# Attention stage of a diffusion layer: transposes into two one-bank buffers, keys loaded by one transfer each, a projection spread over more of the stage

## The chip, the cores and the metric

The kernel runs on one core of a Trainium2 chip. A core has TensorE (matmuls, PE in the profile, its weight loads PEld), VectorE (DVE), ScalarE (ACT), GpSimd (POOL) and SyncE (SP), which here only issues transfers; 16 DMA engines carry all transfers. The metric is the device time of one execution in microseconds (us).

## The reference, cut to what matters

One layer over 1024 tokens and 256 context tokens with 16 heads of 64: an input projection, a recurrent branch, a neighbourhood attention, a merge of the two, and a mixture of 16 experts. The change lies in the attention and in the product of the recurrent branch that is computed beside it:

```python
s_loc = jnp.einsum('bjqhd,brjkhd->bhjqrk', qr, kb).astype(jnp.float32) * scale
s_loc = jnp.where(col_ok[:, :, None, :], s_loc + bias, NEG_INF)
s_ctx = jnp.einsum('bjqhd,bkhd->bhjqk', qr, k_ctx).astype(jnp.float32) * scale
p = jax.nn.softmax(jnp.concatenate([s_loc, s_ctx], axis=-1), axis=-1).astype(v.dtype)
o = (jnp.einsum('bhjqrk,brjkhd->bjqhd', p_loc, vb)
     + jnp.einsum('bhjqk,bkhd->bjqhd', p[..., n_loc:], v_ctx))
...
mix = jax.nn.sigmoid(gr) * (y_rnn @ w_proj_rnn[l]) + jax.nn.sigmoid(gn) * (y_na @ w_proj_na[l])
```

## The kernel before, in words

The stages follow each other: setup and input projections (to about 387 us), the recurrent branch (to 846 us), the attention (846 to 1214 us), the merge, and the experts (from about 1440 us to the end). Every product is made of three fp32r matmuls from high and low parts.

In the attention stage (`stage_attn`) the work is cut into 128 units: 8 pairs of heads, 8 strips of 128 queries, and the 2 heads of the pair. A unit sees 640 keys, or 512 in the first and the last strip; 96 units have 640. `attend` runs one step for each unit n, and the engines take the instructions in the order in which the steps issue them:

- `score(n)`: four matmuls (L905) into `sp`, two PSUM banks wide, of which columns 256 to 895 are used; DVE adds the bias and takes the maximum (L909), then negates it (L911).
- `turn(n - 3)`: four or five transposes on PE (L932) of the softmaxed tile `e` into `pt` (640 columns, two banks, one buffer), and one ACT copy to `et` (L934).
- `values(n - 5)`, at every second step: 20 or 16 matmuls (L949) of two units into `pv`; at the end of each half of a pair ACT and DVE split it (L955, L957) and POOL's queue stores it.
- `expo(n)`: the exponential on ACT (L917). At the next step's start `scale(n - 1)` divides by the sum on DVE (L923, L924).

`load_head` (q: L864; k: L869), `load_bias` (L882) and `load_v` (L876) issue the next pair's loads on SP's queue at steps 2, 4, 6 and 8 of a pair. Of the keys each head has two parts, `k0` and `k1`. A part is 64 rows of 1280 numbers in DRAM (`d_k`) and is wanted twice, in partitions 0 to 63 and 64 to 127: two transfers of 64 partitions each. Four heads fit at a time.

`project` computes the recurrent branch's projection beside it: 2 halves of the tokens by 8 column groups of 24 matmuls into `pr`. Each half begins with four 1 MB loads (`fetch`, L1012), each group needs a 256 KB gate tile (L1021), and each second group takes a 1 MB weight (`S.take8`, ring loads at L90, split by ACT and DVE). `weave` runs whichever of the two generators has the lower running total `done`; so `done` in `project` says at which step of `attend` its pieces of 6 matmuls stand.

Earlier, in the input projections, `out_parts` stores q and k by transfers whose DRAM side has four entries outermost (L484):

```python
nc.sync.dma_start(raw(dst.bitcast(F32), (g * 512 + o + part * 32) * width + tok,
                      [[128 * width, 4], [width, 32], [1, n]]), h[:, :n].bitcast(F32))
```

Of the kernel before, what the change touches and what calls it, by code (L numbers as in the profile page):

```python
# [12 lines left out]
F32 = mybir.dt.float32  # L13
# [12 lines left out]
NT = SEQ + CTX  # L26
# [27 lines left out]

SKIP1, SKIP2 = 7, 7
IDLE = 1
A1, A2 = 3, 4

LRU_ORDER = ([("in", 0)] + [e for j in range(1, 6) for e in (("in", j), ("gate", j - 1))]
# [3 lines left out]
def raw(t, off, dims):  # L63
    return bass.AP(tensor=t.tensor, offset=t.offset + off, ap=dims)
# [109 lines left out]
class Kernel:  # L174
# [142 lines left out]
    def stage_qkv(self):  # L317
# [169 lines left out]
        def mod_rows():  # L487
# [3 lines left out]
            def load(i):  # L491
                if i < 16:
                    ws.append(pl.tile([128, 2048], F32, name="wmr", tag="wmr", bufs=2))
                    nc.gpsimd.dma_start(ws[-1], I["wm"][8 + i])

            load(0)
            load(1)
            for _ in range(IDLE):
                yield
# [348 lines left out]
    def stage_attn(self):  # L848
        nc, I, S = self.nc, self.I, self.S
        self.hip2, self.c_hip2 = self.open_("hip2", side="right", bufs=1)  # L850
        p, cp = self.open_("attn", side="right", bufs=1)
# [4 lines left out]
        ps, cps = self.open_("psa", bufs=1, space=PSUM)  # L856
        L = {}

        def load_head(h):
            if h >= HEADS:  # L860
                return
            pool = pl if h % 4 < 2 else pk
            q = pool.tile([128, SEQ], F32R, name="q", tag="q", bufs=2)
            nc.sync.dma_start(q.bitcast(F32), self.d_q[h].bitcast(F32))  # L864
            ks = []
            for part in range(2):
                t = pool.tile([128, NT], F32R, name=f"k{part}", tag=f"k{part}", bufs=2)
                for x in range(2):
                    nc.sync.dma_start(t[x * 64:(x + 1) * 64].bitcast(F32),  # L869
                                      self.d_k[h, part * 64:(part + 1) * 64].bitcast(F32))  # L870
                ks.append(t)
            L["h", h] = (q, ks)
        def load_v(h):
            if h < HEADS:
                v = (po if h % 4 else pb).tile([128, 10, 128], F32, name="v", tag="v")
                nc.sync.dma_start(v, raw(self.d_v, (h // 2) * 128, [[D, 128], [128 * D, 10], [1, 128]]))  # L876
                L["v", h // 2] = v
# [7 lines left out]
        def keys(s):  # L885

            if s == 0:
                return 256, 0, 512, ((256, 0, 256), (512, SEQ, 256)), (0, 1, 8, 9)
            if s == 7:
                return 256, 896, 512, ((256, SEQ, 256), (512, 6 * 128, 256)), (8, 9, 6, 7)  # L890
            return 256, 256, 640, ((256, SEQ, 256), (512, (s - 1) * 128, 384)), (8, 9, s - 1, s, s + 1)

        units = [(pr, s, i) for pr in range(8) for s in range(8) for i in range(2)]
        state = {}

        def score(n):
            pr, s, i = units[n]
            h = 2 * pr + i
            q, ks = L["h", h]
            b = L["b", h]  # L900
            c0, b0, w, segs, tiles = keys(s)
            sp = ps.tile([128, 1024], F32, name="sp", tag="sp", bufs=2)
            for a, k0, m in segs:
                for part in range(2):
                    nc.tensor.matmul(sp[:, a:a + m], q[:, s * 128:(s + 1) * 128], ks[part][:, k0:k0 + m],  # L905
                                     start=part == 0, stop=part == 1)
            e = p.tile([128, 640], F32, name="e", tag="e", bufs=5)
            mx = p.tile([128, 4], F32, name="mx", tag="mx", bufs=6)
            nc.vector.tensor_tensor_reduce(e[:, :w], sp[:, c0:c0 + w], b[:, b0:b0 + w], 1.0, -3.0e38,  # L909
                                           op0=ALU.add, op1=ALU.max, accum_out=mx[:, 0:1])  # L910
            nc.vector.tensor_scalar(mx[:, 1:2], mx[:, 0:1], -1.0, None, op0=ALU.mult)  # L911
            state[n] = [e, mx]
# [13 lines left out]
        def turn(n):  # L926
            pr, s, i = units[n]
            w = keys(s)[2]
            e, mx = state[n]
            pt = ps.tile([128, 640], F32, name="pt", tag="pt", bufs=1)  # L930
            for c in range(w // 128):
                nc.tensor.transpose(pt[:, c * 128:(c + 1) * 128], e[:, c * 128:(c + 1) * 128], self.ident)  # L932
            et = p.tile([128, 640], F32, name="et", tag="et", bufs=5)
            nc.scalar.copy(et[:, :w], pt[:, :w])  # L934
            state[n] = et

        def values(n):
# [23 lines left out]
        def attend():  # L961
            done = 0.0
            load_head(0)
            load_head(1)
            load_bias(0)
            load_bias(1)
            load_v(0)
            N = len(units)
            for n in range(N + 6):
                if n < N:  # L970
                    h = units[n][0] * 2 + 2
                    if n % 16 == 2:
                        load_head(h)
                    if n % 16 == 4:
                        load_bias(h)
                        load_bias(h + 1)
                    if n % 16 == 6:
                        load_head(h + 1)
                    if n % 16 == 8:
                        load_v(h)  # L980
                    if n == N - 10:
                        cpl.__exit__(None, None, None)
                        cpb.__exit__(None, None, None)
                        self.ring2, self.c_ring2 = self.open_("ring2", bufs=1)
                    if n == N - 1:
                        self.yn = {0: self.fetch_y(0)}
                    score(n)
                    done += 0.55
                if 0 <= n - 3 < N:
                    turn(n - 3)  # L990
                    done += 0.5
                if 0 <= n - 5 < N:
                    values(n - 5)
                    done += 1.2 * (n % 2 == 0)
                if n < N:
                    expo(n)
                yield done
                if 0 <= n - 1 < N:
                    scale(n - 1)

        def project():
            done = 5.0
            yield done
            f = 1.75

            def fetch(hf):

                ys = []
                for part, d in zip("hl", self.d_yr):
                    ys.append(self.halves(part))  # L1010
                    for i, t in enumerate(ys[-1]):
                        nc.sync.dma_start(t.bitcast(F32), raw(d.bitcast(F32), i * 4 * 128 * SEQ + hf * 512,  # L1012
                                                              [[SEQ, 128], [128 * SEQ, 4], [1, 512]]))
                return ys

            tgs = {}

            def fetch_gate(hf, j):
                if hf < 2:
                    tgs[hf, j] = p.tile([128, 512], F32, name="tgl", tag="tgl", bufs=2)  # L1020
                    nc.sync.dma_start(tgs[hf, j], self.d_tgr[j, :, hf * 512:(hf + 1) * 512])  # L1021

            fetch_gate(0, 0)
            for hf in range(2):
                cs = slice(hf * 512, (hf + 1) * 512)
                yh, yl = fetch(hf)
                done += 12.0
                yield done
                for i in range(4):
                    hi, lo = S.take8()  # L1030
                    for x in range(2):
                        j = 2 * i + x
                        xs = slice(x * 128, (x + 1) * 128)
                        tg = tgs.pop((hf, j))
                        fetch_gate(hf + (j + 1) // 8, (j + 1) % 8)
                        pm = ps.tile([128, 512], F32, name="pr", tag="pr", bufs=1)
                        for k in range(8):
                            self.mm3(pm, hi[:, k, xs], lo[:, k, xs], yh[k // 4][:, k % 4], yl[k // 4][:, k % 4],
                                     k == 0, k == 7)
                            if k % 2 == 1:  # L1040
                                done += 0.8 * f
                                yield done
                        m = po.tile([128, 512], F32, name="m1", tag="m1", bufs=2)
                        nc.vector.scalar_tensor_tensor(m, tg, 1.0, pm, op0=ALU.add, op1=ALU.mult)
                        nc.gpsimd.dma_start(self.d_m1[j, :, cs], m)
                        done += 2.0 * f
                        yield done

        weave(attend(), project())
        cps.__exit__(None, None, None)  # L1050
        cpk.__exit__(None, None, None)
# [916 lines left out]
```

## Time and profile before

| | us |
|---|---|
| median of 3 runs (2638.12 to 2643.02) | 2642.32 |
| the profiled execution | 2643.84 |
| its span | 2642.1 |
| attention stage in it, first scores to last values | 846.4 to about 1214.4 |

[...] A busy PE includes overlapping matmuls, so what a step costs is read from the starts of its instructions in the timeline.

### The profile page before, as it was taken

The page shows a single profiled execution, that of the slowest core. Times are in us where ns is not written, and L with a number is a line of the kernel's source. Part 1 is how long each engine was busy: PE and PEld are TensorE (multiplying, and loading weights), DVE is VectorE, ACT ScalarE, POOL GpSimd, SP SyncE. Part 2 cuts the span into 40 slices and gives each one's busy share as a digit, 9 for nine tenths or more (in the row PEclk, how much of TensorE's full clock was granted, in tenths as well). Part 3 has the DMA queues.
Part 4 walks back from the last instruction along what each step waited for, and adds up shares of the span by engine and source line. Part 5 has one row for each costly group of instructions (what it writes and reads, how often), then busy time and mean ns, then how long its engine had stood idle before and what let it go on. Part 6 is the DMA issues. An engine that isn't in the chain of part 4 may idle for free.

```text
span 2642.1 us, 34431 instructions
## 1 busy us (share of the span) xinstructions
PE 2481.3 (94%) x13401; PEld 2040.8 (77%) x13401; DVE 1916.3 (73%) x2294; ACT 1490.3 (56%) x1567; POOL 354.1 (13%) x296
## 2 busy tenths in 40 slices
PE   7999999999998899999987499999999999999996
PEld 4887898777886687777976388888888888888885
DVE  5675643655665566665477789898889888898988
ACT  5321125465655555564333277777777777777776
POOL 1321110121220000000253200000000000000001
PEclk9999999999999999999998699999999999999998
DMA  7455441122206969546865599999999999999985
GB/s 273 147 194 175 168 141 34 66 90 72 102 34 217 293 189 293 181 144 218 274 204 202 201 355 372 373 379 377 372 377 374 374 373 372 373 371 374 373 308 226
DMA packets 260435, 662.86 MB, mean 251 GB/s; under 512 B 18032, under 2 KB 35584, under 8 KB 250544
## 3 DMA queue, kind: packets, MB, share of 16 engines
q1 hardware_dynamic: 236496, 584.13, 62.2%
q0 software_dynamic: 15392, 63.26, 7.1%
q10 hardware_dynamic: 8384, 13.26, 1.6%
q8 instruction: 106, 1.74, 0.3%
q14 instruction: 57, 0.47, 0.1%
HBM read 586.07 MB, written 74.53 MB: 250 GB/s over the span
## 4 chain that ended last, share of the span: by engine, by line
PE 75%; DVE 10%; ACT 7%; DMA 5%; issue 2%; ACTq 0%; POOL 0%; SPq 0%; POOLq 0%; DVEq 0%
PE pm L187 9%; PE pm L188 9%; PE pm L189 9%; PE po L187 4%; PE po L188 4%; PE po L189 4%; PE pp L187 3%; PE pp L188 3%; PE pp L189 3%; PE pv L949 2%; PE pt L932 2%; PE pq L187 2%; PE pq L189 2%; PE pq L188 2%; PE mm L187 2%
## 5 line engine op out<-in xcount | busy, mean ns | idle before, releaser
L98 DVE TENSOR_TENSOR w1l<-ring,w1h 128x2048 fp32r<-128x2048 f32 x150 | 343.5, 2290 | 73.3 <-ACT w1h L181 72.8
L181 ACT CAST w1h<-ring 128x2048 fp32r<-128x2048 f32 x150 | 286.5, 1910 | 86.8 <-PE pm L189 41.0
L98 DVE TENSOR_TENSOR x0l<-ring,x0h 128x2048 fp32r<-128x2048 f32 x105 | 241.5, 2300 | 49.2 <-ACT x0h L181 49.0
L98 DVE TENSOR_TENSOR w0l<-ring,w0h 128x2048 fp32r<-128x2048 f32 x97 | 222.2, 2291 | 69.2 <-ACT w0h L181 67.8
L181 ACT CAST w0h<-ring 128x2048 fp32r<-128x2048 f32 (+1 forms) x100 | 189.2, 1892 | 90.2 <-DMA ring<-wqkv 39.1
L181 ACT CAST x0h<-ring 128x2048 fp32r<-128x2048 f32 x106 | 202.3, 1909 | 55.5 <-PE pm L189 32.9
L1755 POOL DMA_INDIRECT d_acc<-y,idx x15 | 50.3, 3355 | 860.7 <-DVE y L1754 860.7
L909 DVE CUSTOM_DVE_ANT_0 e<-sp,bias 128x640 f32<-128x640 f32 (+1 forms) x128 | 100.7, 787 | 81.0 <-PE sp L905 71.8
L187 PE MATMUL pm<-w0h,xeh 128*128 128x512 f32 x384 | 154.6, 403 | 0.0
L188 PE MATMUL pm<-w0l,xeh 128*128 128x512 f32 x384 | 152.7, 398 | 0.0
L189 PE MATMUL pm<-w0h,xel 128*128 128x512 f32 x384 | 152.6, 397 | 0.0
L934 ACT COPY et<-pt 128x640 f32<-128x640 f32 (+1 forms) x128 | 84.8, 663 | 105.3 <-PE pt L932 103.5
L187 PE MATMUL pm<-x0h,xeh 128*128 128x512 f32 x320 | 128.3, 401 | 0.0
L187 PE MATMUL pm<-w1h,xeh 128*128 128x512 f32 x320 | 127.7, 399 | 0.0
L188 PE MATMUL pm<-x0l,xeh 128*128 128x512 f32 x320 | 126.7, 396 | 0.4 <-DVE x0l L98 0.4
L917 ACT ACTIVATE e<-e,mx 128x640 f32<-128x640 f32 (+1 forms) x128 | 103.0, 805 | 42.5 <-DVE mx L911 41.4
L189 PE MATMUL pm<-w1h,xel 128*128 128x512 f32 x320 | 126.8, 396 | 0.0
L188 PE MATMUL pm<-w1l,xeh 128*128 128x512 f32 x320 | 126.7, 396 | 0.0
L189 PE MATMUL pm<-x0h,xel 128*128 128x512 f32 x320 | 126.2, 394 | 0.0
L187 PE MATMUL pp<-xh,w1h 128*128 128x512 f32 (+1 forms) x304 | 116.2, 382 | 3.9 <-ACT tg L730 3.2
L188 PE MATMUL pp<-xl,w1h 128*128 128x512 f32 (+1 forms) x304 | 115.8, 381 | 0.0
L189 PE MATMUL pp<-xh,w1l 128*128 128x512 f32 (+1 forms) x304 | 115.7, 381 | 0.0
(458 smaller groups left out, 6922.5 us busy)
## 6 DMA issues: line engine op xcount, KB each, us to landing
ring<-w_exp_down SPq DMA_DIRECT2D x104, 1024.0 KB
ring<-w_exp_gate SPq DMA_DIRECT2D x101, 1024.0 KB
ring<-w_exp_up SPq DMA_DIRECT2D x100, 1024.0 KB
k<-d_k SPq DMA_DIRECT2D x64, 320.0 KB
wmr<-wm POOLq DMA_DIRECT2D x16, 1024.0 KB, 8.9
ring<-wrnn SPq DMA_DIRECT2D x16, 1024.0 KB
ring<-wqkv SPq DMA_DIRECT2D x12, 1024.0 KB
bias<-bias SPq DMA_DIRECT2D x16, 704.0 KB
```

The costliest lines, as they stand in the source:

```text
L98: (engine or self.lo_engine).tensor_sub(lo, x, hi)
L181: self.nc.scalar.copy(hi, x)
L187: mm(out, wh, xh, start=first, stop=False)
L188: mm(out, wh, xl, start=False, stop=False)
L189: mm(out, wl, xh, start=False, stop=last)
L909: nc.vector.tensor_tensor_reduce(e[:, :w], sp[:, c0:c0 + w], b[:, b0:b0 + w], 1.0, -3.0e38, op0=ALU.add, op1=ALU.max, accum_out=mx[:, 0:1])
L917: nc.scalar.activation(e[:, :w], e[:, :w], AF.Exp, bias=mx[:, 1:2], accum_out=mx[:, 2:3])
L932: nc.tensor.transpose(pt[:, c * 128:(c + 1) * 128], e[:, c * 128:(c + 1) * 128], self.ident)
L934: nc.scalar.copy(et[:, :w], pt[:, :w])
L949: nc.tensor.matmul(pv[j * 64:(j + 1) * 64, (s % 4) * 128:(s % 4 + 1) * 128], v[:, t, j * 64:(j + 1) * 64], state[n - 1 + j][:, c * 128:(c ...
L1755: nc.gpsimd.indirect_dma_start(out=self.d_acc[:, :], out_offset=bass.IndirectOffsetOnAxis(ap=self.idx[:, e:e + 1], axis=0), in_=y[:, :], i ...
```

## The change: what it does

- `turn` runs four steps behind the scores instead of three. Its tile `pt` is 512 columns, one bank, in two buffers. The fifth transpose of a 640-wide unit goes into columns 0 to 127 of the `sp` tile that `score` filled at the same step; a second ACT copy takes it to `et`. In the last four steps it gets an `sp` tile of its own.
- A part of the keys is loaded by one transfer of 128 partitions whose DRAM side is `[[0, 2], [NT, 64], [1, NT]]`: the outermost entry runs over the two copies, with step 0.
- `project` starts at 0 instead of 5: its first loads are issued after unit 0; its first matmuls come after 27 instead of 12 more, and each piece counts 2.1 instead of 1.75, so that the pieces spread to the end of the stage.

```diff
@@ load_head
-                for x in range(2):
-                    nc.sync.dma_start(t[x * 64:(x + 1) * 64].bitcast(F32),
-                                      self.d_k[h, part * 64:(part + 1) * 64].bitcast(F32))
+                nc.sync.dma_start(t.bitcast(F32), raw(self.d_k.bitcast(F32), (h * 128 + part * 64) * NT,
+                                                      [[0, 2], [NT, 64], [1, NT]]))
@@ score
-            sp = ps.tile([128, 1024], F32, name="sp", tag="sp", bufs=2)
+            sp = L["sp"] = ps.tile([128, 1024], F32, name="sp", tag="sp", bufs=2)
@@ turn
-            pt = ps.tile([128, 640], F32, name="pt", tag="pt", bufs=1)
+            pt = ps.tile([128, 512], F32, name="pt", tag="pt", bufs=2)
+            et = p.tile([128, 640], F32, name="et", tag="et", bufs=5)
             for c in range(w // 128):
-                nc.tensor.transpose(pt[:, c * 128:(c + 1) * 128], e[:, c * 128:(c + 1) * 128], self.ident)
-            et = p.tile([128, 640], F32, name="et", tag="et", bufs=5)
-            nc.scalar.copy(et[:, :w], pt[:, :w])
+                if c == 4 and n + BEHIND >= len(units):
+                    L["sp"] = ps.tile([128, 1024], F32, name="sp", tag="sp", bufs=2)
+                o = pt[:, c * 128:(c + 1) * 128] if c < 4 else L["sp"][:, 0:128]
+                nc.tensor.transpose(o, e[:, c * 128:(c + 1) * 128], self.ident)
+            nc.scalar.copy(et[:, :512], pt)
+            if w > 512:
+                nc.scalar.copy(et[:, 512:], o)
@@ attend
-                if 0 <= n - 3 < N:
-                    turn(n - 3)
+                if 0 <= n - BEHIND < N:
+                    turn(n - BEHIND)
@@ project
-            done = 5.0
+            done = 0.0
-            f = 1.75
+            f = 2.1
...
-                done += 12.0
+                done += 27.0 if hf == 0 else 6.0
```

SP's queue where the attention's loads begin, before: keys (`k`, two transfers in a row marked x2) and queries of heads 0 and 1, then biases, values, and the loads of heads 2 and 3.

```order
L869 DMA k_6408<-d_k 64x1280 x2
L869 DMA k_6411<-d_k 64x1280 x2
L864 DMA q<-d_q 128x1024
L869 DMA k_6416<-d_k 64x1280 x2
L869 DMA k_6419<-d_k 64x1280 x2
L882 DMA bias<-bias 128x1408 x2
L876 DMA v<-d_v 128x10x128
L864 DMA q<-d_q 128x1024
L869 DMA k_6452<-d_k 64x1280 x2
```

SP's queue from the same key load on, after.

```order
L870 DMA k_6408<-d_k 128x1x1280
L870 DMA k_6410<-d_k 128x1x1280
L866 DMA q<-d_q 128x1024
L870 DMA k_6414<-d_k 128x1x1280
L870 DMA k_6416<-d_k 128x1x1280
L884 DMA bias<-bias 128x1408 x2
L878 DMA v<-d_v 128x10x128
L1029 DMA tgl<-d_tgr 128x512
L1020 DMA x0h<-d_yrh 128x4x512
L1020 DMA x1h<-d_yrh 128x4x512
```

The four 1 MB loads of the recurrent branch (two of them shown) now stand ahead of the loads of heads 2 and 3, and the keys have half as many transfers.

PE's queue at an even step of a 640-wide unit, before: `sp` are the scores, `pt` the transposes, `pv` the values; the names in brackets are the engines whose progress the instruction waits for.

```order
L905 MATMUL sp<-k_6408,q 128x256 [waits DVE_49]
L905 MATMUL sp<-k_6411,q 128x256
L905 MATMUL sp<-k_6408,q 128x384
L905 MATMUL sp<-k_6411,q 128x384
L932 MATMUL pt<-ident,e 128x128 [waits DVE_49,Activation_49]
L932 MATMUL pt<-ident,e 128x128 x4
L949 MATMUL pv<-et,v 64x128 x10
```

PE's queue at such a step, after.

```order
L907 MATMUL sp<-k_6408,q 128x256 [waits Activation_49]
L907 MATMUL sp<-k_6410,q 128x256
L907 MATMUL sp<-k_6408,q 128x384
L907 MATMUL sp<-k_6410,q 128x384
L939 MATMUL pt<-ident,e 128x128 [waits PE_49]
L939 MATMUL pt<-ident,e 128x128 x3
L939 MATMUL sp<-ident,e 128x128 [waits DVE_49]
L957 MATMUL pv<-et,v 64x128
L957 MATMUL pv<-et,v 64x128 [waits Activation_49]
```

The fifth transpose now stands alone with a wait for DVE; the count that it waits for in the built program is the one that DVE reaches with the bias-and-maximum instruction (L909 before, L911 after) of the same step's scores. Nothing stands between the scores, the four transposes and it; the projection's pieces stand between steps.

## Rows read from the trace of the kernel before

**Rows 1.** The page: busy time, share of the span and instructions of each engine.

```profile
PE 2481.3 (94%) x13401; PEld 2040.8 (77%) x13401; DVE 1916.3 (73%) x2294; ACT 1490.3 (56%) x1567; POOL 354.1 (13%) x296
```

**Rows 2.** Windows over the attention stage: stretch, length, busy times, clock, DMA share, GB/s.

```profile
846.40:860.00 13.60, 7.21 (x31) 6.12 (x32) 5.96 (x20) 4.22 (x10) 0.00 (x0) 0.55 1.01 289
...
878.00:892.00 14.00, 4.47 (x14) 3.38 (x14) 4.78 (x10) 3.58 (x6) 0.79 (x2) 0.64 1.04 371
892.00:1161.00 269.00, 255.44 (x2045) 213.02 (x2044) 170.36 (x489) 152.85 (x292) 20.06 (x37) 1.00 0.74 224
1161.00:1214.00 53.00, 47.96 (x481) 39.56 (x479) 37.22 (x122) 38.16 (x77) 3.79 (x7) 1.00 0.33 115
```

**Rows 3.** Waits in the stage: who waited for whom, us in total, times, longest.

```profile
PEld pt L932 <- ACT et L934: 25.8, 42, 1.1
...
PE pr L188 <- DMA x0l<-d_yrl: 5.8, 1, 5.8
```

**Rows 4.** Timeline of PE, two steps without projection: start, length, instruction, wait.

```profile
1169.83 0.71 PE L905 MATMUL sp<-k,q 128*128 128x256 f32 x4
1170.91 0.76 PE L932 MATMUL pt<-ident,e 128*128 128x128 f32 x5 [0.37 <-ACT et L934]
1171.60 1.31 PE L949 MATMUL pv<-et,v 128*64 128x128 f32 x20
1172.85 0.73 PE L905 MATMUL sp<-k,q 128*128 128x256 f32 x4
1173.42 0.71 PE L932 MATMUL pt<-ident,e 128*128 128x128 f32 x5
1173.88 0.72 PE L905 MATMUL sp<-k,q 128*128 128x256 f32 x4
...
1176.90 0.74 PE L905 MATMUL sp<-k,q 128*128 128x256 f32 x4
```

**Rows 5.** Timeline of DVE in the first of these steps.

```profile
1170.68 0.82 DVE L909 CUSTOM_DVE_ANT_0 e<-sp,bias 128x640 f32<-128x640 f32 x1
```

**Rows 6.** Windows: key and query stores (L484), key loads (L869), recurrent loads (L1012).

```profile
87.00:106.00 19.00, 18.14 (x103) 14.91 (x102) 11.52 (x16) 9.29 (x14) 10.51 (x12) 1.00 0.26 101
...
828.00:832.00 4.00, 4.00 (x19) 3.20 (x18) 3.93 (x4) 0.22 (x1) 0.00 (x0) 1.00 1.03 235
874.00:880.00 6.00, 3.85 (x38) 2.91 (x36) 4.13 (x14) 4.51 (x9) 1.09 (x2) 1.00 1.04 348
```

**Rows 7.** SP's queue during those stores: first and last of eight issues.

```profile
83.69 0.51 SPq L484 DMA_DIRECT2D d_k<-ohi  x1
...
94.66 2.46 SPq L484 DMA_DIRECT2D d_q<-olo  x1
```

**Rows 8.** SP's queue: the attention's first load, and its first bias loads.

```profile
824.12 0.33 SPq L864 DMA_DIRECT2D q<-d_q  x1
...
846.24 0.82 SPq L882 DMA_DIRECT2D bias<-bias  x2
```

**Rows 9.** Transfers issued from 840 to 1220 us: how many, KB each.

```profile
k<-d_k SPq DMA_DIRECT2D x56, 320.0 KB
bias<-bias SPq DMA_DIRECT2D x16, 704.0 KB
q<-d_q SPq DMA_DIRECT2D x14, 512.0 KB
...
v<-d_v SPq DMA_DIRECT2D x8, 640.0 KB
tgl<-d_tgr SPq DMA_DIRECT2D x16, 256.0 KB
```

**Rows 10.** ACT's queue from 832 to 850 us: packets, MB, share of 16 engines.

```profile
q10 hardware_dynamic: 1028, 2.40, 35.5%
```

**Rows 11.** Timeline of PE: projection matmuls, ten starts apart.

```profile
894.02 0.40 PE L188 MATMUL pr<-x0l,w0h 128*128 128x512 f32 x1
...
896.36 0.39 PE L189 MATMUL pr<-x1h,w0l 128*128 128x512 f32 x1
```

More of the change, by code (lines that the diff above doesn't have):

```diff
@@ L56 @@
 IDLE = 1
+BEHIND = 4
 A1, A2 = 3, 4
```

## The prediction

> **What bounds the kernel now.** I read the page first: PE is busy for 94% of the span [rows 1], so what TensorE waits for in the attention stage is what the change can win or lose. Then the windows of the stage [rows 2]. Two stretches stand out: 846.4 to 860 and 878 to 892, where PE is busy for only 7.2 of 13.6 and 4.5 of 14 us, the clock is granted at a mean of 0.55 and 0.64, and the DMA engines are full (1.01 and 1.04). The first is the stage's start, which waits for its biases; in the second the projection's first matmuls wait for the recurrent branch's loads [rows 3] with the scores queued behind them. The other 322 us are the steady part. There PE waits for ACT to empty the one `pt` buffer, 25.8 us in 42 waits [rows 3]. The timeline shows one: scores at 1169.83 take PE until about 1170.4, the next transposes start at 1170.91 after ACT's copy, values at 1171.60, next scores at 1172.85 [rows 4]. This even step lasts 3.02 us, of which about 0.5 is that wait; the odd one behind it 1.03, to 1173.88.
>
> So PE decides the stage; the DMA engines are at 0.74 of their time in the mixed part and 0.33 at its end [rows 2], which looks like room.
>
> **The sum.** I make it against the profiled execution, 2643.84 us with a span of 2642.1 (the median is 1.5 us lower).
>
> *Loading earlier, multiplying later.* The first loads of the recurrent branch leave after unit 0 and their first matmuls come at step 19 instead of 13. The stretch from 878 to 892 would lose its idle 9.5 us and the low clock behind it: a gain of 8 to 14 us, if the loads of heads 2 and 3, now behind those 4 MB, are there in time.
>
> *Two `pt` buffers.* The wait for ACT's copy goes: up to 25.8 us. ACT's added copies (96 of 128 columns) cost nothing while ACT is busy for 38 of 53 us at the end and less before [rows 2]; without that cover each would be part of the 0.69 us copy.
>
> *The fifth transpose.* It waits for DVE to have read the scores of its own step. Scores start at 1169.83, DVE's L909 starts at 1170.68 when they are through and ends 0.82 later, at 1171.50 [rows 4, 5]. So the fifth can't start before 1.67 us into the step; the scores and four transposes need 0.57 + 4 x 0.09 = 0.93 (1172.85 to 1173.42, and a fifth of 1173.42 to 1173.88 for each transpose). PE is in order, so values, projection and the next scores are queued behind: 0.7 us in each of 94 steps (96 units less two with a tile of their own), 66 us. DVE must be free when the scores are; where it splits a weight it isn't, for which I found no row and allow up to 2 us at each of eight weights. By itself this takes away more than the two gains give: 66 - 26 - 11 = 29 us.
>
> [...]
>
> *The keys.* Here the trace speaks against the change. From 87 to 106 us almost all traffic is the eight stores of L484 [rows 7], whose DRAM side has four entries outermost, and the share of the DMA engines is 0.26 at 101 GB/s [rows 6]: four engines out of 16 at 25.3 GB/s each. It isn't the small packets: the recurrent loads, with rows of 2 KB too, reach 1.04 and 348 GB/s, and the keys in their present form, 64 rows outermost, 1.03 and 235 [rows 6]. So the number of entries outermost sets how many engines work, if it is below 16. The new transfer has two. I expect two engines: 2 x 320 KB [rows 9] is 655,360 B, 327,680 per engine, 13.0 us at 25.3 GB/s, against 2.8 us now at 235 GB/s. No row shows two engines, a DRAM read or a step of 0. The other end for the rate is the present loads' 235 / 16 = 14.7 GB/s per engine, 22.3 us each; I take 25.3 since there too few engines worked.
>
> [...]
>
> What that does: all loads of SP's queue pass through these two engines in order, each with a sixteenth on each of them. So I add what one of the two has to move from the first load at 824.1 [rows 8] until the last head's keys are there, at 25.3 GB/s, sizes from rows 9:
>
> - 32 key transfers x 13.0 = 416 us;
> - 16 queries x 1.3 (512 KB / 16), 16 biases x 1.8, 7 values x 1.6, 13 gate tiles x 0.65: 69 us;
> - 6 weights and 8 recurrent loads, 1 MB each by their shapes, x 2.6: 36 us;
> - from other queues: ACT's 2.40 MB at the stage's start [rows 10], 6 us, and POOL's 256 KB stores, some 41 of them x 0.65, 27 us.
>
> That is 554 us, so the last keys land at about 1378. It has no idle time in it: a pair of heads asks for 4 x 13.0 + 2.6 + 3.6 + 1.6 and some 7.8 of the rest, 67 us, while PE needs for 16 steps 8 x (1.03 + 3.02) plus 48 projection matmuls x 0.234 [rows 11], 44 us, or some 49 with the fifth's waits. So PE waits for keys at every pair, by nearly 20 us, at a low clock after each wait, and the gains above are lost in these waits. SP isn't held up: when PE starts a pair's second unit, the next loads' buffers have been free for a pair.
>
> After the last keys come unit 113 and the rest. Before, unit 113's scores start at 1176.90 [rows 4] and the stage ends at 1214.4: 37.5 us. To this come 48 projection matmuls, 11 us, which now stand there, and 11 fifth transposes x 0.7 less 5 copies' waits x 0.5, 5 us: 54. The stage ends at 1378 + 54 = 1432 instead of 1214.4, 217 us later. At a rate 5% higher the 554 would be 528, and the end 191 later. I take a little under the first, **210 us**: 2643.84 + 210 = 2853.8, and 1.5 less for the median: **2852**.
>
> **The rivals.**
>
> *All 16 engines take the keys* (the rule read from the stores doesn't hold for reads with a step of 0). Then the loads keep their cover, and the fifth transpose decides: 29 us, or up to 45 with weight splits in DVE's way: 2643.84 + 29 = 2673. For it: no row shows such a read. Against it: the stores are the same form with the sides exchanged.
>
> *Faster: the keys on 16 engines, and the fifth's wait is mostly covered*, because PE comes to it late anyway. It decides below (26 + 11) / 94 = 0.39 us a step; at 0.2 it costs 19, and 37 - 19 = 18 us are won: 2626. For it: two buffers and a spread projection fill PE's waits. Against it: nothing stands between scores and fifth transpose that could be late, and 1.67 - 0.93 is made of lengths of rows.
>
> *Much slower: two engines at 14.7 GB/s.* 32 x (22.3 - 13.0) = 298 us more than forecast: 3150. For it: the present key loads are that slow per engine; against it: with all 16 at work the limit may be shared, and the stores show 25.3.
>
> **How the numbers follow.** Forecast (two engines, about 25 GB/s) 0.84; 16 engines and slower 0.08; faster 0.04; much slower 0.04. The range takes the rate from 10% above 25.3 (50 less than forecast) to 11% below (62 more; the recurrent loads have 348 / 16 = 21.8 per engine with all 16 at work [rows 6]): 2800 to 2915, which leaves out the rivals and a little of the forecast, under 2 in 10. About 0.2% is what a measurement of this kernel can tell: faster 0.04, same 0.01 (the first rival at its lower end), slower 0.95.
>
> **What would show it.** Right: DMA share near 0.13 to 0.2 for long stretches of the stage with PE idle on `sp` for `k` or `q` loads, about 15 to 30 us at each new pair; the first bias-and-maximum on DVE near 885, some 39 us after the bias loads are issued [rows 8]; the stage some 210 us longer and the stages after it as long as before. The fifth transpose: a wait of about 0.7 us for L911 in each 640-wide step, none for `et` of any weight. Wrong: key loads at a DMA share near 1, the stage below 410 us; or idle PE for another reason than keys.

## The result: 2900.91 us, slower by 9.7%

The kernel after takes 2900.91 us (median of 4 runs, 2899.97 to 2902.16) beside 2642.67 us for the kernel before on the same chip: a ratio of 1.0973, with a 95% interval from 1.0958 to 1.0988. The prediction was 2852 us in a range from 2800 to 2915. The profiled execution has a span of 2900.4 us against 2642.1.

The page of the kernel after: busy times, TensorE's granted clock (tenths of full speed) and the busy share of the 16 DMA engines (tenths) in 40 slices of the span, and the chain that ended last. The first row answers to [rows 1].

```profile
PE 2521.8 (87%) x13401; PEld 2064.0 (71%) x13401; DVE 1919.2 (66%) x2294; ACT 1500.9 (52%) x1663; POOL 357.9 (12%) x296
...
PEclk9999999999987788879899979999999999999998
DMA  7554431122035333343357648999999999999995
...
PE 64%; DMA 14%; DVE 10%; ACT 6%; SPq 3%; issue 2%; ACTq 0%; POOL 0%; POOLq 0%; DVEq 0%
DMA k<-d_k 11%; PE pm L189 8%; PE pm L190 8%; PE pm L191 8%; PE po L189 4%; PE po L191 4%; PE po L190 4%; PE pp L189 2%; PE pp L190 2%; PE pp L191 2%; PE pq L189 2%; PE pq L191 2%; PE pq L190 2%; PE mm L189 2%; PE mm L191 2%
```

PE has the same 13401 instructions and is busy for 87% of the span instead of 94%. Key loads alone are 11% of the chain, some 320 us. The clock is below 0.9 in slices 12 to 18 and 20 (a slice is 72.5 us), which lie in the attention stage, with the DMA engines at 0.3 to 0.5, and besides only in slices 24 and 40, behind the stage.

The DMA engines from 940 to 980 us in 40 slices of 1 us (busy share in tenths, GB/s):

```profile
DMA  1111111111179611111111111861110111111111
GB/s 44 51 51 51 51 56 51 51 51 51 69 211 302 169 43 56 73 51 51 51 51 51 51 51 50 296 245 44 44 46 28 54 51 54 46 51 51 51 51 51
```

51 GB/s at a tenth of the engines is what the key transfers get; the bursts between, with shares up to 0.9 and 302 GB/s, are other loads.

Windows of the kernel after, with the columns of [rows 2]: the main part of the stage, and all that follows it.

```profile
892.00:1161.00 269.00, 170.89 (x1220) 137.44 (x1220) 112.77 (x327) 105.34 (x239) 10.81 (x20) 0.81 0.39 133
...
1474.00:2899.00 1425.00, 1341.22 (x6504) 1099.02 (x6502) 1193.43 (x1055) 903.40 (x713) 178.59 (x98) 0.97 0.92 332
```

From 892 to 1161 us PE does 1220 matmuls where it did 2045 before, at a clock of 0.81 of full speed instead of 1.00. The stage ends at 1473.3 us (first matmul behind it) instead of 1214.6, 258.7 us later. What follows takes 1427 us in both. So all of the loss is in this stage.

What PE waited for in the stage of the kernel after (us in total, times, longest):

```profile
PE sp L907 <- DMA k<-d_k: 124.9, 13, 15.4
PE sp L939 <- DVE mx L911: 65.3, 87, 4.3
PE pr L189 <- DMA x0h<-d_yrh: 40.7, 1, 40.7
PE sp L907 <- ACT tg L732: 16.3, 1, 16.3
PE pr L190 <- DMA x0l<-d_yrl: 4.6, 1, 4.6
```

The first row is the keys, the second the fifth transposes (L939 into `sp`), the third one single wait for the second half of the recurrent branch, the fourth the wait at the stage's start. The waits for `et` of [rows 3] are gone. The last heads' keys end PE's last long wait:

```profile
1414.43 1.01 PE L907 MATMUL sp<-k,q 128*128 128x256 f32 x3 [13.14 <-DMA k<-d_k]
```

SP's queue before that 40.7 us wait (start, length of the issue, what it issues):

```profile
1208.68 17.10 SPq L870 DMA_DIRECT2D k<-d_k  x2
1225.88 12.22 SPq L878 DMA_DIRECT2D v<-d_v  x1
1238.45 13.63 SPq L1020 DMA_DIRECT2D x0h<-d_yrh  x1
1252.19 1.16 SPq L1020 DMA_DIRECT2D x1h<-d_yrh  x1
```

SP stands still nowhere between these rows: the issues themselves take that long, and the recurrent loads leave 30 to 47 us after the keys ahead of them. Over all key loads, first of the kernel after and then of the kernel before (shortest, median and longest issue in ns):

```profile
L870 SPq DMA_DIRECT2D k<-d_k x32: 492/2400/18258, 823.6 to 1366.6; - x32
```

```profile
L869 SPq DMA_DIRECT2D k<-d_k x64: 444/594/1336, 824.5 to 1143.4; - x64
```

One issue takes up to 18.3 us instead of 1.3, though the median is only 2.4: at such issues SP is held up, in a stretch (826.1 to 1413.9) in which some packet was under way in all but 3 of 588 us.

### The profile page after: what moved, and what is told of

The parts are those of the page before. It is cut to its first block, busy times and chain, and to the rows that moved or that the text cites. A ratio compares the mean times of both kernels' runs of the same rounds, so it can differ in the third digit from the quotient of the medians.

```text
span 2900.4 us, 34359 instructions
## 1 busy us (share of the span) xinstructions
PE 2521.8 (87%) x13401; PEld 2064.0 (71%) x13401; DVE 1919.2 (66%) x2294; ACT 1500.9 (52%) x1663; POOL 357.9 (12%) x296
## 4 chain that ended last, share of the span: by engine, by line
PE 64%; DMA 14%; DVE 10%; ACT 6%; SPq 3%; issue 2%; ACTq 0%; POOL 0%; POOLq 0%; DVEq 0%
DMA k<-d_k 11%; PE pm L189 8%; PE pm L190 8%; PE pm L191 8%; PE po L189 4%; PE po L191 4%; PE po L190 4%; PE pp L189 2%; PE pp L190 2%; PE pp L191 2%; PE pq L189 2%; PE pq L191 2%; PE pq L190 2%; PE mm L189 2%; PE mm L191 2%
## 5 line engine op out<-in xcount | busy, mean ns | idle before, releaser
L100 DVE TENSOR_TENSOR w1l<-ring,w1h 128x2048 fp32r<-128x2048 f32 x150 | 343.4, 2289 | 72.5 <-ACT w1h L183 71.9
L911 DVE CUSTOM_DVE_ANT_0 e<-sp,bias 128x640 f32<-128x640 f32 (+1 forms) x128 | 101.0, 789 | 327.3 <-PE sp L907 269.4
L100 DVE TENSOR_TENSOR x0l<-ring,x0h 128x2048 fp32r<-128x2048 f32 x105 | 240.6, 2292 | 50.0 <-ACT x0h L183 49.7
L100 DVE TENSOR_TENSOR w0l<-ring,w0h 128x2048 fp32r<-128x2048 f32 x97 | 222.2, 2290 | 73.3 <-ACT w0h L183 71.9
L907 PE MATMUL sp<-k,q 128*128 128x256 f32 (+1 forms) x512 | 111.6, 341 | 143.1 <-DMA k<-d_k 124.9
L940 ACT COPY et<-pt 128x512 f32<-128x512 f32 x128 | 74.5, 582 | 306.6 <-PE pt L939 306.5
L907 PEld LDWEIGHTS sp<-k,q 128*128 128x128 f32 x512 | 82.1, 211 | 157.9 <-DMA k<-d_k 93.7
```

What stands on the lines that cost most here:

```text
L100: (engine or self.lo_engine).tensor_sub(lo, x, hi)
L940: nc.scalar.copy(et[:, :512], pt)
```

## The experiments

Each kernel is named by its label; line numbers in its rows are its own. Ratios are against the kernel before on the same chip, with 95% intervals. "The kernel after" is the changed kernel of this case.

### The three parts, each by itself

**e1_halves** is the kernel after, with the key loads of before.

```diff
-                nc.sync.dma_start(t.bitcast(F32), raw(self.d_k.bitcast(F32), (h * 128 + part * 64) * NT,
-                                                      [[0, 2], [NT, 64], [1, NT]]))
+                for x in range(2):
+                    nc.sync.dma_start(t[x * 64:(x + 1) * 64].bitcast(F32),
+                                      self.d_k[h, part * 64:(part + 1) * 64].bitcast(F32))
```

> The kernel after with one thing undone: the keys come again in two transfers of 64 partitions each. My theory (only two DMA engines carry the new key transfer, and apart from that the fifth transpose costs PE a wait in every 640-wide step): the attention stage loses nearly all of its extra time, and what stays is the fifth transpose net of the earlier loads, 2673 us (2660 to 2690); PE's waits for key loads are gone, the fifth's waits for L911 of about 0.5 to 0.8 us stay. Rival 1 (the fifth's wait is covered in a full stage): 2626, below the kernel before. Rival 2 (the long stage comes from the order of the transposes and the projection, not from the keys): it stays above 2850.

Measured: 2713.23 us, ratio 1.0265 (1.0244 to 1.0286). 188 of the 258 us are the key loads. But what stays is 69 us and not my 29, outside the range that I gave it. PE's waits in its stage, a window, and the sums over the stage of this kernel and (last row) of the kernel before, each from 846.4 us to the stage's end:

```profile
PE sp L940 <- DVE mx L912: 69.9, 93, 4.3
...
892.00:1161.00 269.00, 221.79 (x1697) 180.12 (x1695) 148.29 (x420) 139.33 (x309) 16.81 (x31) 0.96 0.62 188
...
sum 435.40, PE 354.73 PEld 287.65 DVE 235.72 ACT 226.65 POOL 25.35; mean PE 88.68 PEld 71.91 DVE 58.93 ACT 56.66 POOL 6.34
```

```profile
PE pt L932 <- ACT et L934: 9.6, 30, 0.8
PE pt L932 <- DVE e L924: 8.1, 9, 1.8
...
sum 368.10, PE 332.19 PEld 276.13 DVE 231.98 ACT 212.93 POOL 25.35; mean PE 66.44 PEld 55.23 DVE 46.40 ACT 42.59 POOL 5.07
```

The stage is 67.3 us longer (435.4 less 368.1). PE stands idle for 80.7 us instead of 35.9, 44.8 more, and the same instructions keep it busy for 354.7 instead of 332.2, 22.5 more. The idle part adds up: the fifths' waits bring 69.9, the waits for `et` and `e` take away 9.6 + 8.1, the waits for the recurrent loads (3.7 + 5.8 us before) take away 9.5, which gives 42.7. The busy part has two sources of about the same size. One is the clock. The windows in which it was granted at 0.50 sum to 24.0 us in the kernel before (first row; two stretches) and to 44.3 us in this one (seven stretches):

```profile
sum 24.00, PE 11.86 PEld 9.86 DVE 10.51 ACT 6.05 POOL 0.00; mean PE 5.93 PEld 4.93 DVE 5.26 ACT 3.02 POOL 0.00
...
sum 44.30, PE 34.86 PEld 28.10 DVE 18.87 ACT 15.23 POOL 1.05; mean PE 4.98 PEld 4.01 DVE 2.70 ACT 2.18 POOL 0.15
```

PE is busy in them for 23.0 us more. If that work takes half as long at 1.00 as at 0.50 (20 matmuls of the values, shown below, take 1.31 us instead of 2.40), the clock brings 11.5 us (an estimate). The other source is the way in which busy time is counted: PE has some 50 pauses more (93 waits against 30 + 9 in the rows above), and before each the last transpose ends with nothing running under it. Four transposes that start 0.09 us apart last 0.60 us, so 0.24 us a pause, some 12 us (an estimate too).

A weight split shows what a long wait does (timeline of PE):

```profile
1133.91 0.33 PE L940 MATMUL sp<-ident,e 128*128 128x128 f32 x1 [0.49 <-DVE mx L912]
...
1140.94 0.47 PE L940 MATMUL sp<-ident,e 128*128 128x128 f32 x1 [4.26 <-DVE mx L912]
1141.34 2.40 PE L958 MATMUL pv<-et,v 128*64 128x128 f32 x20
1143.68 0.80 PE L189 MATMUL pr<-x0h,w1h 128*128 128x512 f32 x1
1144.27 0.63 PE L190 MATMUL pr<-x0l,w1h 128*128 128x512 f32 x1
```

DVE at the same time:

```profile
1137.19 2.29 DVE L100 TENSOR_TENSOR w0l<-ring,w0h 128x2048 fp32r<-128x2048 f32 x1 [3.14 <-ACT w0h L183]
```

At 1133.91 stands the ordinary wait, 0.49 us. At 1140.94 DVE has first waited 3.14 us for ACT's half of a weight split, then made its own (2.29 us), and PE's wait is 4.26; behind it the 20 matmuls of the values take 2.40 instead of 1.31 us and a projection matmul 0.63 instead of 0.39, until the clock is back. Two windows of the same stretch give the granted clock: 1.00 before that wait, 0.50 behind it.

```profile
1125.00:1136.00 11.00, 8.86 (x63) 7.20 (x64) 5.43 (x16) 5.74 (x15) 0.54 (x1) 1.00 0.49 189
...
1141.00:1146.00 5.00, 5.00 (x27) 3.98 (x28) 0.70 (x3) 1.08 (x3) 0.00 (x0) 0.50 0.00 0
```

Of the 93 waits, 18 are of 0.8 us and more and make 36 us; the other 75 make 33. Seven of the long ones, 20.6 us, stand directly behind a weight split (L100); in the others DVE was late with other work, such as the split of `pv` (L966) or the gate's product (L1053). The clock fell at 6 of the 18, 5 of them behind weight splits, for 3.4 to 6.8 us each.

**e2_keys_only** is the other way round: the kernel before with only the new key loads (the diff above, with + and - exchanged).

> The kernel before with only the key loads changed to the one transfer per half with a leading step of 0. My theory: the two engines carry the same sum of bytes as in the kernel after, so the last keys land near 1400 us and the stage ends some 40 us later: 2860 to 2900 us, with 51 GB/s and a DMA share of 0.13 while only keys move. Rival (the keys cost this much only together with the later projection and the fifth transposes): 2700 or less.

Measured: 2889.76 us, ratio 1.0929 (1.0910 to 1.0949). A window in which only keys move:

```profile
930.00:940.00 10.00, 0.00 (x0) 0.00 (x0) 0.00 (x0) 0.00 (x0) 0.00 (x0) 0.50 0.13 52
```

As expected: 2 of 16 engines (0.13), 52 GB/s, and 245 of the 258 us by the keys alone.

**e7_schedule** is the kernel before with only the projection's schedule of the kernel after.

```diff
-            done = 5.0
+            done = 0.0
             yield done
-            f = 1.75
+            f = 2.1
...
-                done += 12.0
+                done += 27.0 if hf == 0 else 6.0
```

> The kernel before with only the projection's schedule changed (starts at 0, first matmuls after 27, spread at 2.1). My theory: the waits for the recurrent loads near 880 us go, with the low clock behind them: a gain of 8 to 14 us, 2630 to 2636. Rival (projection matmuls that filled PE's waits early in the stage now stand late, and PE waits as much elsewhere): 2640 to 2650.

Measured: 2649.93 us, ratio 1.0027 (1.0016 to 1.0038). No gain; a small loss. The waits of PE for loads in its stage:

```profile
PE sp L905 <- DMA k<-d_k: 4.1, 2, 2.2
PE pr L188 <- DMA x0l<-d_yrl: 3.4, 1, 3.4
```

The 9.5 us of [rows 3] and its partner row have turned into 4.1 us for the second pair's keys, which now stand behind the 4 MB, and 3.4 us for the second half's loads. Waits for loads thus fall by only 2 us, while those at the transposes (for ACT and DVE) rise from 17.7 to 21.4. The window from 892 to 1161 has 1996 matmuls instead of 2045 and a clock of 0.98.

**e8_transposes** is the kernel before with only the transposes of the kernel after (tiles `pt`, `et`, the fifth in `sp`, and four units behind).

> The kernel before with only the transposes changed (two one-bank buffers, four units behind, the fifth in its own step's scores tile), so that each part of the change has been run alone. Theory (the fifth's waits and the clock lost by them make up nearly all that the kernel with two key transfers lost, and the schedule alone cost 7): 2713 - 7 = 2706, between 2698 and 2712. Rival (the fifth's waits cost so much only with the projection spread out): 2670 to 2690, near my 29 us.

Measured: 2716.07 us, ratio 1.0285 (1.0266 to 1.0304), 74 us slower and 4 above the upper end that I gave. So the 69 us of e1_halves come from the transposes with either schedule, and the rival falls. The parts alone give 245 + 74 + 7 = 326 us, together 258. That fits a fifth transpose's wait costing less while PE waits for keys anyway, but no run isolates it.

### How many engines a transfer gets

**e3_interleaved** keeps one transfer of 128 partitions and the step of 0, but not outermost; the queries follow the same order of rows.

```diff
-                                                      [[0, 2], [NT, 64], [1, NT]]))
+                                                      [[NT, 64], [0, 2], [1, NT]]))
```

> The kernel after, with the keys still in one transfer of 128 partitions per half and each row still read twice by a step of 0, but with the 64 rows outermost and the step of 0 inside; the queries are loaded in the matching order of rows. Theory (the number of entries in the outermost dimension sets how many engines work): 16 engines, key loads at a share near 1, time as with two transfers of 64 partitions, 2660 to 2690. Rival (it is the step of 0, or 128 partitions in one transfer, that is slow): 51 GB/s as in the kernel after, 2850 to 2905.

Measured: 2716.05 us, ratio 1.0273 (1.0254 to 1.0292), the time of e1_halves, 26 us above my figure for the same reason as there.

**e5_two_outer** has no step of 0 and two transfers, but two entries outermost (the queries in four transfers of 32 rows to match).

```diff
-                nc.sync.dma_start(t.bitcast(F32), raw(self.d_k.bitcast(F32), (h * 128 + part * 64) * NT,
-                                                      [[0, 2], [NT, 64], [1, NT]]))
+                for x in range(2):
+                    nc.sync.dma_start(t[x * 64:(x + 1) * 64].bitcast(F32),
+                                      raw(self.d_k.bitcast(F32), (h * 128 + part * 64) * NT,
+                                          [[NT, 2], [2 * NT, 32], [1, NT]]))
```

> The kernel after, with keys in two transfers of 64 partitions without any step of 0, but each read as 2 outermost entries of 32 rows (even rows, then odd ones); queries are loaded in the matching order. Theory (outermost entries): again two engines, 51 GB/s while only keys move, 2880 to 2920 us. Rival (the step of 0 or the 128 partitions): 16 engines, 2660 to 2690.

Measured: 2916.89 us, ratio 1.1034 (1.1008 to 1.1060), as the theory had it.

**e6_eight_outer** is the same with `[[NT, 8], [8 * NT, 8], [1, NT]]`, and the queries with 8 entries outermost.

> The kernel after, with keys in two transfers of 64 partitions that read 8 outermost entries of 8 rows each, queries likewise. Theory (as many engines as outermost entries): 8 engines, about 200 GB/s and a DMA share near 0.5 while only keys and queries move, 3.2 us for 640 KB, hidden behind a pair of heads: 2700 to 2730 us, as with 64 outermost. Rival (anything but 64 rows outermost falls back to two engines): above 2850.

Measured: 2738.22 us, ratio 1.0357 (1.0338 to 1.0375), 8 us above the upper end; PE waits here 7.2 us for keys and 8.6 for the recurrent loads. One window of each of the three, early in the key loads of the first heads (e3, e6) and at the second pair's (e5):

```profile
828.00:832.00 4.00, 4.00 (x19) 3.23 (x18) 3.97 (x3) 0.74 (x2) 0.00 (x0) 1.00 0.97 321
```

```profile
931.00:947.00 16.00, 4.64 (x28) 3.64 (x28) 1.41 (x5) 1.56 (x4) 0.00 (x0) 0.50 0.13 52
```

```profile
831.00:836.00 5.00, 5.00 (x24) 4.00 (x23) 4.90 (x4) 0.00 (x0) 0.00 (x0) 1.00 0.51 143
```

64, 2 and 8 outermost entries give shares of 0.97, 0.13 and 0.51: 16, 2 and 8 engines. With the four of [rows 6] (0.26) that is four sizes on one line. Neither the step of 0 nor the 128 partitions takes engines away (e3 has both, at 0.97); the place of the entry of 2 in the pattern does (e5 has neither, at 0.13). My 200 GB/s for eight engines was wrong: 143, 18 GB/s each, against 26 each for two. With 16 engines the form matters too: in the same stretch, mostly key loads, e3 moves 321 GB/s, 20 per engine, the kernel before 235, 14.7 per engine [rows 6]. So the one transfer with the step of 0 inside is the faster one, though the time of the kernel doesn't show it. Why it is faster, and why eight engines are slower each than two, no run shows. With 64 entries outermost, one transfer (e3) and two (e1) give the kernel the same time, 2716.05 and 2713.23 us.

**e4_pool_queue** issues the keys from POOL (`nc.gpsimd` for `nc.sync`), in the form of the kernel after.

> The kernel after, with the 32 key transfers issued by POOL instead of SP; their form stays (leading step of 0). It tells what SP's being held up costs: in the kernel after SP takes 11 to 19 us to issue one key transfer while the two engines have work queued, and the loads of biases, values, gates and the recurrent branch wait behind. Theory A (the sum on two engines decides, SP's hold-up adds little): still two engines, 2880 to 2910 us. Theory B (the hold-up adds PE's 41 us wait for the recurrent loads and the late biases): 2830 to 2870. If POOL's queue spreads the rows over all engines, the keys cost nothing and it gives the 2713 us of the kernel with two transfers.

Measured: 2750.31 us, ratio 1.0402 (1.0383 to 1.0421). Neither theory. A window in which little but keys moves:

```profile
970.00:976.00 6.00, 6.00 (x45) 5.06 (x45) 2.35 (x7) 2.23 (x6) 0.00 (x0) 1.00 0.26 95
```

The share, 0.26 instead of 0.13, is that of four engines, which I read as the two transfers of a head at the same time on two engines each; the trace doesn't number the engines, so no run shows which they were. All but 37 us of the 188 are back. Since the number of engines differs as well as the issuing queue, this run doesn't say what SP's being held up costs. That stays open.

### Where the fifth transpose can stand

**e9_late_fifth** has the keys in two transfers and moves the fifth transposes to where DVE has read the scores: of an even unit behind the values, in the step's own `sp`; of an odd unit one step later, in the `sp` of the step before. `e` gets six buffers instead of five, `et` four instead of five.

```diff
+            if n % 2 == 0 and n > 0:
+                fifth(n - 1, L["sp1"])
             nc.scalar.copy(et[:, :512], pt)
...
                     values(n - 5)
+                if n % 2 == 0 and 0 <= n - BEHIND < N:
+                    fifth(n - BEHIND, L["sp"])
```

> The kernel after with keys in two transfers and the fifth transpose moved to where DVE has long read the scores: for the even unit of a pair behind the values of the same step, into that step's scores tile; for the odd unit one step later, behind four transposes, into the scores tile of the step before. Theory (the fifth's wait and the clock lost by it make up all of the 2713 us beside the gains): the waits for L912 at the fifth vanish, the waits for the one buffer too, and the gains of two buffers and earlier loads are left: 2605 to 2625 us, faster than the kernel before by about 1%. Rival (ACT's two copies per unit or DVE take the place as the limit): 2640 to 2660.

Measured: 2644.89 us, ratio 1.0002 (0.9993 to 1.0011), 20 us above my upper end and in the rival's range. The new place is worth 68 us (2713 less 2645), but no gain over the kernel before is left. PE's waits say why:

```profile
PE sp L945 <- DVE mx L913: 21.2, 15, 3.1
PE sp L909 <- DMA k<-d_k: 7.8, 2, 5.7
```

DVE is still late at 15 fifths, and the keys behind the early recurrent loads still come late.

**e11_later_loads** is the kernel before with the recurrent loads issued after the second pair's, and **e12_late_fifth_loads** is e9_late_fifth with the same schedule.

```diff
-            done = 5.0
+            done = 10.0
             yield done
-            f = 1.75
+            f = 1.95
...
-                done += 12.0
+                done += 27.0 if hf == 0 else 10.0
```

> The kernel before with the recurrent loads issued after the second pair's loads, as in the kernel with paired fifths, and its matmuls from 37 on, spread at 1.95. Theory (the first part of the stage is short of DMA, so loading earlier only makes the keys late, but loading later, for matmuls that come later, takes the wait away): PE's 9.5 us of waits near 880 and 3 to 4 us of low clock go: 2628 to 2636. Rival (these waits come back elsewhere, as with the earlier loads): 2640 to 2650.

Measured: 2638.72 us, ratio 0.9981 (0.9972 to 0.9990): a gain of 4.4 us, between the two theories. The waits for loads are gone; those for DVE grew from 8.1 to 12.4 us.

> The kernel with late fifth transposes, and of the other edits only the recurrent loads after the second pair's loads. Theory: 2645 less the 8 us that PE waits for keys near 885, 1.6 us for the second half's loads and some 4 us of low clock: 2628 to 2636. Rival: no change, 2640 to 2650.

Measured: 2646.16 us, ratio 1.0009 (0.9999 to 1.0018): no change against e9_late_fifth, as the rival had it. The wait for keys went, and the wait for DVE rose from 21.2 to 28.1 us:

```profile
PE sp L945 <- DVE mx L913: 28.1, 18, 4.8
```

**e10_pair_fifth** takes that schedule and puts both fifths of a pair side by side into the `sp` of the step before, in the even step behind the four transposes.

```diff
+            late = [m for m in (n - 1, n) if n % 2 == 0 and m > 0 and keys(units[m][1])[2] > 512]
+            o = {m: L["sp1"][:, (m - n + 1) * 128:(m - n + 2) * 128] for m in late}
+            for m in late:
+                nc.tensor.transpose(o[m], state[m][1][:, 512:640], self.ident)
```

> The late fifth transposes, with both of a pair (even and odd unit) in one place: in the even step behind four transposes, side by side in the scores tile of the step before; and the recurrent loads issued after the second pair's keys, biases and values, their matmuls from 37 on, spread at 1.95. Theory (in the kernel with late fifths DVE's weight splits still cost 21 us of waits at the fifths, and the first keys behind the recurrent loads 8 us and low clock): most of both goes, 2610 to 2625 us, faster than the kernel before by about 1%. Rival (the waits only move on to the next reader of DVE or DMA): 2638 to 2650.

Measured: 2626.68 us, ratio 0.9940 (0.9926 to 0.9953), faster than both kernels, by 16 us than the kernel before; my upper end was 2 us too low. A pair of steps in the timeline of PE, and its waits in the stage:

```profile
866.07 0.85 PE L909 MATMUL sp<-k,q 128*128 128x256 f32 x4
866.76 0.60 PE L936 MATMUL pt<-ident,e 128*128 128x128 f32 x4
867.12 0.83 PE L909 MATMUL sp<-k,q 128*128 128x256 f32 x4
867.79 0.60 PE L936 MATMUL pt<-ident,e 128*128 128x128 f32 x4
868.22 0.38 PE L941 MATMUL sp<-ident,e 128*128 128x128 f32 x2
868.53 1.31 PE L964 MATMUL pv<-et,v 128*64 128x128 f32 x20
869.78 0.85 PE L909 MATMUL sp<-k,q 128*128 128x256 f32 x4
```

```profile
PE sp L941 <- DVE mx L913: 13.2, 11, 3.5
```

Two steps take 3.71 us (866.07 to 869.78) with no wait in them, against 4.05 before [rows 4] and 5.12 in the kernel after:

```profile
1206.21 0.83 PE L907 MATMUL sp<-k,q 128*128 128x256 f32 x4
...
1211.33 0.83 PE L907 MATMUL sp<-k,q 128*128 128x256 f32 x4
```

The fifths wait 13.2 us instead of 28.1. Against e12_late_fifth_loads, which has the same loads, the pairing alone gives 19 us.

## Why the prediction was right, and where its steps failed

**Two engines, about 25 GB/s each: right.** 51 GB/s in the pure stretches of the kernel after, and 0.13 of the engines at 52 GB/s in e2 and e5. PE's waits for keys, 124.9 us in 13, come to some 16 us for each of the eight pairs, at the lower end of the 15 to 30 that were named. The step from the stores' four entries to the loads' two is confirmed by e2, e3, e5 and e6, not only by the total.

**The serial sum, 554 us from 824.1 to 1378: right in form, 36 us short.** The last keys were there at 1414.4. From the first key packet (826.1) to the last (1413.9) are 588 us, and in all but 3 of them some packet was under way, so "it has no idle time in it" held. The packets of SP's queue fill this time. The keys' packets of 5,120 B took 216 ns in the mean, and 200 where only keys move; that is 443 us on each of the two engines instead of 416. A sixteenth of the queue's other packets, the share of one engine, is 145 us instead of 105 (69 + 36): I had priced them at 25.3 GB/s per engine, but the biases' packets of 5,632 B took 308 ns in the mean (18 GB/s) and those of 512 B, most of them the values', 37 ns (14 GB/s). Together that is the 588. It leaves nothing for the 33 us that I had added for ACT's and POOL's queues; I take it that their packets ran alongside. So two terms were 67 us too small and one of 33 was too much, and that they partly cancel is luck. The last keys of most pairs landed 71 to 73 us behind those of the pair before instead of 67, with 79 once and 87 once. The range has a slip of its own: a rate 11% lower makes 554 / 0.89 = 622, 68 us more and not 62.

**"SP isn't held up": wrong.** It was, by up to 18.3 us in one issue. It changed which load PE waited for: the 40.7 us for the second half's recurrent loads, where I had expected waits of 15 to 30 us for keys only. Whether it changed the time can't be told: the two engines had work all along, which speaks for little; no run isolates it.

**The stage's end: 54 us after the last keys expected, 59 measured.** With 36 from the sum, 5 from here, and the 7 that I had rounded off (217 to 210), that is the 48 us by which 258 exceeds 210. The stages behind are as long as before, as forecast. The first bias-and-maximum came at 890.5, expected near 885:

```profile
872.59 0.81 SPq L884 DMA_DIRECT2D bias<-bias  x2
...
890.52 0.69 DVE L911 CUSTOM_DVE_ANT_0 e<-sp,bias 128x512 f32<-128x512 f32 x1 [44.72 <-DMA bias<-bias]
```

That it came so near is luck: I had the bias loads issued at 846 and landing 39 us later. SP issued them at 872.6, after waiting 10.4 us for the recurrent branch's last stores and 6.8 for keys, and they landed 18 us later.

**The fifth transpose: total right, parts and net wrong.** 69.9 us of waits in e1_halves where the sum had 66 for 94 steps. But an ordinary wait is 0.35 or 0.49 us and not 0.7, and 18 long ones make 36 us. For the weight splits I had set aside at most 16 us; the 7 waits behind them make 20.6, and the other long ones, behind other work of DVE, had no term. The net, 29 us, was the step that failed: 69 to 74. The largest part had no term at all: PE's busy time rises by 22.5 us, by the estimates above about half of it by the low clock at some of the waits and half by the many pauses. Next, 25.8 us for the wait on `pt` was the row of the weight loads [rows 3]; PE's own rows, shown with e1_halves, have 9.6, and 8.1 more on DVE. Last, the 11 us for earlier recurrent loads. Beside the fifth transposes their 9.5 us of waits do go (e1_halves), but by itself the schedule makes the kernel 7 us slower (e7_schedule); e1_halves and e8_transposes, which differ in it alone, are 5 us apart, and their intervals overlap. I had written the condition down ("if the loads of heads 2 and 3, now behind those 4 MB, are there in time") and taken it as met; in e7_schedule they were not. In the kernel after nearly all of this is hidden behind the keys (it takes 2901 us, e2_keys_only 2890), so it hardly moved the forecast; had the keys had 16 engines, my 2673 would have been 40 us too low.

**"None for `et` of any weight": right**; and the rival that the fifth's wait is covered has fallen with e1_halves and e8_transposes.

## What to carry to other kernels

Read the outermost entry of a transfer's DRAM side before its size: with 2 there, the keys here got a share of 0.13 of the engines and 52 GB/s, and the loads behind them on SP's queue came late too (one wait of 40.7 us for the recurrent branch); with the repeated dimension inside (e3_interleaved) one transfer cost no more than two. A transpose into a tile that another engine still reads, even in other columns, is priced at that engine's worst steps too (here DVE's weight splits, 20.6 us in 7 waits of e1_halves, and the clock of 0.50 behind 5 of them), not only at its usual one; put it where a whole step lies between (13.2 us of waits in e10_pair_fifth instead of 69.9). And a load moved ahead in a queue that is full can cost the loads behind it what it gains (e7_schedule: 7 us slower).

## What the runs showed of the hardware

- An issue on SP's queue has no fixed price: 0.4 to 1.3 us for a key load before, up to 18.3 us with the key transfers of the kernel after ahead, while in the pure stretches (share 0.13) 14 of 16 engines had nothing to do.
- The same transfers issued from POOL (e4_pool_queue) had a share of 0.26, that of four engines, at 95 GB/s, where SP's had 0.13, that of two, at 52 GB/s (e2_keys_only): 2750 us instead of 2901.
- The rate of one engine isn't fixed. For keys it was 26 GB/s with two engines at work (e2, e5) and 18 with eight (e6); with sixteen it was 14.7 in two transfers of 64 partitions (the kernel before) and 20 in one of 128 with the step of 0 inside (e3).
- In e1_halves, behind a single wait of 4.26 us, the granted clock stood at 0.50 for about 5 us, and 20 matmuls took 2.40 us instead of 1.31. At 12 of the 18 waits of 0.8 us and more it didn't fall.
